# A row of 1,024 gains through DRAM: one write and one broadcast read in place of eight transposes in a hybrid block

## The chip, the cores and the metric

The kernel runs on one core of one Trainium2 chip. The metric is the device time of one execution in microseconds (us). Before the change it is 730.49 us, the median of three runs (730.33 to 730.49).

## The reference, cut to what matters

One backbone layer over 512 latent tokens of width 1,024, with 256 context tokens. A modulation vector gives shift, scale and gate; the normed input goes through one wide projection; a gated convolution and a neighbourhood attention of 16 heads are projected, merged through two gates, projected once more, normed and added to the input:

```
sh, sc, gt = _modulation(c, w_mod[i], b_mod[i])
h = _rmsnorm(x, pre_g[i]) * (1.0 + sc[:, None, :]) + sh[:, None, :]
parts = _split_in(h @ w_in[i])
...
merged = sigmoid(g_a) * y_a + sigmoid(g_b) * y_b
y = merged @ w_o
x = x + gt[:, None, :] * _rmsnorm(y, post_g[i])
```

The last line is what the change touches: each of the 1,024 output columns is multiplied by `gt * post_g` of that column. Both are vectors over columns, the same for every token.

## The kernel before, in words

All matmuls are on TensorE (PE) in fp32r, with operands split into a high part (a ScalarE cast, L70) and a low part (a VectorE subtraction, L71); a projection of one unit is three matmuls (L115, L116, L117) for each of eight slices of the contraction. Weights come in chunks of two DMAs of 512 KB each (`Chunk`, L84, tile `raw`, two buffers), issued by SyncE (SP) one chunk ahead of their use.

The work has these stages:

- **Start and context.** Modulation columns, norm, the first projection with its weights, then context keys and convolutions 0 to 3. `gain(k)` (L447 to L455) computes eight columns of the gate as a [128, 8] tile, `gains`: column 128k + p of the model lies in partition p, place k. L466 multiplies them with the post norm weight.
- **Eight pairs of heads** (the loop at L664). `blocks` holds for each pair two heads with four blocks of 128 queries; eight slots a pair. Each slot takes pieces of the projections listed in `plan` (keys and queries, values, convolutions, gates), then scores, softmax, transposes and the product with the values. The bias tile `bt` is loaded for each half pair (L543).
- **Merge** (the loop at L710). For j = 0 to 7 the two branch projections of unit j are multiplied with their gates and added; merge gates of unit j + 2 follow (L719). At j = 5 the products of gate and post norm weight are brought from [128, 8] columns to a tile that every partition holds in full, `gpost` [128, 1024]: eight copies on VectorE spread a column over 128 places (L730, tile `ta`), eight transposes on PE against the identity turn each so that every partition has the row (L731), and two ScalarE copies empty the two PSUM banks (L732). At j = 6 the output projection's first half of weights is loaded and split (`load_wo`, L705, tile `wo`).
- **Output projection** (L745 on). PE multiplies (L754); ScalarE sums the squares (L759), VectorE multiplies with `gpost` (L760); after the norm's root VectorE scales and adds `x` (L791), and the result is stored (L794).

Outside a part of the start that is written as a manual schedule, the framework orders each engine's instructions: an instruction is placed when its inputs and its buffers are ready, with the order of the program as priority. So one can run far ahead of its place in the text. Each engine and each DMA queue then works in that order. PSUM banks of the merge come in turn from eight (`pj`); tiles of the merge's pool `bp`, `gpost` among them, take the memory that the attention's pool `aw` gives back.

Of the kernel before, what the change touches and what calls it, by code (L numbers as in the profile page):

```python
# [9 lines left out]
F32 = mybir.dt.float32  # L10
# [5 lines left out]
P = 128  # L16
D = 1024
KT = 8
S = 512
# [8 lines left out]
def layer(ctx: ExitStack, tc, xp, ctxt, ctxT, cc, wmod, small, wfirst, win, wout, wo, rel, tab, out):  # L28
    nc = tc.nc
# [3 lines left out]
    wp = ctx.enter_context(tc.tile_pool(name="wp", bufs=2))  # L33
    cv = ctx.enter_context(tc.tile_pool(name="cv", bufs=2))
    pp = ctx.enter_context(tc.tile_pool(name="pp", bufs=1, space=bass.MemoryType.PSUM))

    class Banks:

# [9 lines left out]
    ident = const.tile([P, P], F32, name="ident")  # L48
# [4 lines left out]
    gains = const.tile([P, KT], F32, name="gains")  # L53
# [13 lines left out]
    def split(H, L, src, scale=None):  # L67

        if scale is None:
            nc.scalar.copy(H, src)  # L70
            nc.vector.tensor_sub(L, src, H.bitcast(F32))  # L71
        else:
            nc.scalar.mul(H, src, scale)
            nc.vector.scalar_tensor_tensor(
                out=L, in0=src, scalar=scale, in1=H.bitcast(F32), op0=ALU.mult, op1=ALU.subtract
            )
# [150 lines left out]
    pj = Banks(0, 1, 2, 3, 4, 5)  # L227

    def unit(w, i, m=hx):
        ps = pj()  # L230
        proj_T(ps, w, i, m)
        return ps
# [346 lines left out]
    def turn2(pts, b, TH, TL):  # L579
        tps = [psT().rearrange("p (c q) -> p c q", c=4) for _ in pts]  # L580
        for tp, pt in zip(tps, pts):
            for c in range(4):
                nc.tensor.transpose(tp[:, c], pt[:, c * P:(c + 1) * P], ident)  # L583
        for n, tp in enumerate(tps):
            split(TH[:, b + n], TL[:, b + n], tp)

    def gather(p, h, TH, TL):
        r, q = (lo, hi)[h], (hi, lo)[h]
        o = psO()
        o3 = o.rearrange("p (b q) -> p b q", b=4)  # L590

        work = [(4, slice(0, 4), lambda t: t[:, :, 2]), (5, slice(0, 4), lambda t: t[:, :, 3])]
        work.append((0, slice(0, 4, 3), lambda t: t[:, 0:4:3, 0]))
        for k in range(1, 3):
            work.append((k, slice(k - 1, k + 1), lambda t, k=k: t.rearrange("p b c q -> p (b c) q")[:, 4 * k - 3:4 * k + 1:3]))
        work.append((3, slice(2, 4), lambda t: t[:, 2:4, 1]))
        for n, (kt, dst, src) in enumerate(work):
            for t in (TH, TL):
                nc.tensor.matmul(  # L599
                    o3[:, dst], lhsT=V[p][:, kt, h], rhs=src(t),  # L600
                    start=n == 0 and t is TH, stop=n == len(work) - 1 and t is TL,
                )
        tmp = aw.tile([P, S], F32, name="tmp", bufs=1)
        nc.scalar.copy(tmp[r], o[q])
        nc.vector.tensor_add(attn[p][r, 64:512], o[r, :448], tmp[r, :448])
        nc.vector.tensor_add(attn[p][r, 0:64], o[r, 448:], tmp[r, 448:])
# [19 lines left out]
    def merge_gates(j):  # L626
        w = chunk()
        G[j] = []
        for i in range(2):
            n = 2 * j + i  # L630
            g = hp.tile([P, S], F32, name=f"g{n}", tag=f"hc{n % 8}")
            nc.scalar.activation(g, unit(w, i), AF.Tanh, scale=0.5)  # L632
            G[j].append(g)
            yield

    def chain(*gs):
        for g in gs:
            yield from g
# [24 lines left out]
    done = 0  # L663
    for i, (p, h, b) in enumerate(blocks):  # L664
        slot = i % 8
        if slot == 0:
            items = chain(*(g for g, _ in fill[p]))
            total, done = sum(n for _, n in fill[p]), 0
        upto = -(-total * (slot + 1) // 8)
        while done < upto:  # L670
            next(items)
            done += 1
        if T is not None and b == 0:
            gather(*T)
        if i + 2 < len(blocks):
            pts[i + 2] = scores(*blocks[i + 2])
        if b == 0:
            TH = aw.tile([P, 4, 4, P], F32R, name="TH", bufs=1)
            TL = aw.tile([P, 4, 4, P], F32R, name="TL", bufs=1)
            T = p, h, TH, TL  # L680

        if b % 2:
            turn2([pts.pop(i - 1), pts.pop(i)], b - 1, TH, TL)
# [7 lines left out]
    pj = Banks(*range(8))  # L691
# [9 lines left out]
    def load_wo(c, H, L):  # L701

        for i in range(4):
            raw = wp.tile([P, 2, S], F32, name="raw", bufs=2)
            nc.sync.dma_start(raw, wo[c, :, 2 * i:2 * i + 2])  # L705
            for k in range(2):
                split(H[2 * i + k], L[2 * i + k], raw[:, k])
        return H, L

    for j in range(KT):  # L710
        w = chunk()
        g = G[j]
        for i in range(2):
            nc.vector.scalar_tensor_tensor(  # L714
                out=g[i], in0=g[i], scalar=1.0, in1=unit(w, i, ua[i]), op0=ALU.add, op1=ALU.mult
            )
        nc.vector.tensor_add(g[0], g[0], g[1])
        split(mm[0][j], mm[1][j], g[0], 0.5)
        if j < 6:  # L719
            for _ in merge_gates(j + 2):  # L720
                pass
        if j == 5:

            gpost = bp.tile([P, D], F32, name="gpost")
            for i in range(2):
                gb = cv.tile([P, S], F32, name="ta")
                ps = pj()
                for k in range(4):
                    n = 4 * i + k
                    nc.vector.tensor_copy(gb[:, k * P:(k + 1) * P], gains[:, n:n + 1].broadcast_to([P, P]))  # L730
                    nc.tensor.transpose(ps[:, k * P:(k + 1) * P], gb[:, k * P:(k + 1) * P], ident)  # L731
                nc.scalar.copy(gpost[:, i * S:(i + 1) * S], ps)  # L732
        if j == 6:

            t = [hp.tile([P, 2, S], F32R, name=f"wo{i}", tag=f"h{i}") for i in range(8)]
            wos = [load_wo(0, [x[:, i] for x in t[:4] for i in range(2)], [x[:, i] for x in t[4:] for i in range(2)])]
# [8 lines left out]
    for c in range(2):  # L745
        H, L = wos[c]
        cs = slice(c * S, (c + 1) * S)
        ps = [pj() for t in range(4)]
# [129 lines left out]
```

## Time and profile before

| | |
|---|---|
| median of three runs | 730.49 us |
| profiled execution | 730.42 us |
| its span, first to last instruction | 728.6 us |
| granted TensorE clock, mean | 0.999 |
| PE busy | 716.9 us |
| VectorE (DVE) busy | 515.2 us |
| ScalarE (ACT) busy | 331.9 us |
| HBM read and written | 83.93 MB and 2.10 MB |

The profile is of one execution; 1.8 us lie outside its span. Rows of instructions name line, engine, operation, output and inputs; a row of the DMA queue of SyncE is named SPq. In the chain that ended last, each piece starts when what it waited for was done, so its starts give the pace of the engine, while busy times of matmuls overlap one another.

### The profile page before, as it was taken

What the parts mean: (1) busy time and instruction counts of PE and PEld (TensorE: products, weight loads), DVE (VectorE), ACT (ScalarE), POOL (GpSimd) and SP (SyncE); (2) the same over time, 40 slices, a digit from 0 to 9 for tenths busy, and PEclk for the clock granted to TensorE, in tenths of its full rate; (3) what the DMA queues carried; (4) which work ended last, traced back from release to release, by engine and by line L of the source; (5) the groups of instructions that cost most, each with busy time, mean ns of one, the idle gap of its engine ahead of it and who ended that gap; (6) DMA issues with size and microseconds to landing.
All of it is one profiled execution on the core that took longest, in us unless ns stands there. A gap on an engine that the chain in (4) does not pass through costs nothing.

```text
span 728.6 us, 9358 instructions
## 1 busy us (share of the span) xinstructions
PE 716.9 (98%) x3512; PEld 601.9 (83%) x3512; DVE 515.2 (71%) x1060; ACT 331.9 (46%) x619; POOL 0.7 (0%) x6
## 2 busy tenths in 40 slices
PE   7999999999999999999999999999999999999996
PEld 4888888888888888888888888888888888888885
DVE  6979999996998968879879779675844324335323
ACT  6564533563464654555536446434823213314221
POOL 0000000000000000000000000000000000000000
PEclk9999999999999999999999999999999999999999
DMA  8984973223212222121322212322133133235402
GB/s 343 406 305 175 317 269 121 96 67 99 72 60 73 72 74 73 58 88 57 116 73 73 73 58 73 98 77 73 58 115 109 65 116 103 71 116 181 165 10 107
DMA packets 25967, 86.63 MB, mean 119 GB/s; under 512 B 3009, under 2 KB 3393, under 8 KB 25922
## 3 DMA queue, kind: packets, MB, share of 16 engines
q1 hardware_dynamic: 25778, 85.84, 34.0%
q8 instruction: 27, 0.44, 0.2%
q10 hardware_dynamic: 144, 0.20, 0.1%
q14 instruction: 18, 0.15, 0.1%
HBM read 83.93 MB, written 2.10 MB: 118 GB/s over the span
## 4 chain that ended last, share of the span: by engine, by line
PE 96%; DVE 1%; DMA 1%; ACT 1%; SPq 0%; issue 0%; DVEq 0%; ACTq 0%
PE ps L115 20%; PE ps L117 20%; PE ps L116 20%; PE ps L128 6%; PE ps L754 6%; PE ps L599 4%; PE ps L583 4%; PE ps L133 3%; PE ps L551 3%; PE ps L141 2%; PE ps L307 2%; PE ps L311 2%; PE ps L308 2%; DMA wm<-in_wmod 1%; PE ps L560 1%; PE ps L146 1%
## 5 line engine op out<-in xcount | busy, mean ns | idle before, releaser
L115 PE MATMUL ps<-h,w 128*128 128x512 f32 x528 | 207.5, 393 | 0.0
L117 PE MATMUL ps<-h,w 128*128 128x512 f32 x528 | 206.0, 390 | 0.0
L116 PE MATMUL ps<-h,w 128*128 128x512 f32 x528 | 205.7, 390 | 0.0
L71 DVE TENSOR_TENSOR w<-raw,w 128x1024 fp32r<-128x1024 f32 (+1 forms) x98 | 113.1, 1173 | 58.9 <-ACT w L70 58.7
L70 ACT CAST w<-raw 128x1024 fp32r<-128x1024 f32 (+1 forms) x98 | 96.9, 1016 | 93.4 <-PE ps L117 64.6
L117 PEld LDWEIGHTS ps<-h,w 128*128 128x128 f32 x528 | 99.1, 188 | 20.9
L116 PEld LDWEIGHTS ps<-h,w 128*128 128x128 f32 x528 | 99.2, 188 | 20.2
L115 PEld LDWEIGHTS ps<-h,w 128*128 128x128 f32 x528 | 99.2, 188 | 20.1
L574 ACT ACTIVATE pt<-ps,m 128x512 f32<-128x512 f32 x64 | 44.3, 694 | 59.0 <-DVE m L571 59.0
L567 DVE CUSTOM_DVE_ANT_1 ps<-ps,bt 128x512 f32<-128x512 f32 x56 | 38.6, 700 | 15.1 <-PE ps L551 12.0
L71 DVE TENSOR_TENSOR TL<-ps,TH 128x512 fp32r<-128x512 f32 x64 | 42.7, 680 | 5.2 <-ACT TH L70 5.2
L714 DVE SCALAR_TENSOR_TENSOR g<-g,ps 128x512 f32<-128x512 f32 x16 | 11.0, 687 | 42.3 <-PE ps L117 42.3
L70 ACT CAST TH<-ps 128x512 fp32r<-128x512 f32 x64 | 35.1, 588 | 6.6 <-PE ps L583 6.4
L632 ACT ACTIVATE g<-ps 128x512 f32<-128x512 f32 x16 | 9.6, 598 | 59.6 <-PE ps L117 59.6
L583 PE MATMUL ps<-ident,pt 128*128 128x128 f32 x256 | 33.3, 272 | 0.0
L128 PE MATMUL ps<-w,h 128*128 128x512 f32 x128 | 32.7, 395 | 0.0
L576 DVE TENSOR_SCALAR pt<-pt,z 128x512 f32<-128x512 f32 x64 | 30.8, 482 | 1.0
L583 PEld LDWEIGHTS ps<-ident,pt 128*128 128x128 f32 x256 | 29.4, 140 | 2.3
L599 PE MATMUL ps<-TH,V 128*128 128x256 f32 (+1 forms) x96 | 28.5, 319 | 0.0
L599 PE MATMUL ps<-TL,V 128*128 128x256 f32 (+1 forms) x96 | 27.7, 318 | 0.0
L516 ACT ACTIVATE qd<-ta 64x512 fp32r<-64x512 f32 x32 | 20.2, 631 | 14.3 <-PE ps L560 7.6
L128 PEld LDWEIGHTS ps<-w,h 128*128 128x128 f32 x128 | 23.1, 189 | 4.3
(158 smaller groups left out, 1133.1 us busy)
## 6 DMA issues: line engine op xcount, KB each, us to landing
raw<-in_win SPq DMA_DIRECT2D x74, 512.0 KB, 4.2
wm<-in_wmod SPq DMA_DIRECT2D x34, 512.0 KB, 6.8
raw<-in_wout SPq DMA_DIRECT2D x16, 512.0 KB, 4.0
bt<-in_rel SPq DMA_DIRECT2D x16, 256.0 KB, 2.6
raw<-in_wo SPq DMA_DIRECT2D x8, 512.0 KB, 3.7
fraw<-in_wfirst SPq DMA_DIRECT2D x8, 384.0 KB, 8.1
x<-in_xp SPq DMA_DIRECT2D x4, 512.0 KB, 5.3
xr<-in_xp SPq DMA_DIRECT2D x4, 512.0 KB, 5.9
```

The costliest lines, as they stand in the source:

```text
L70: nc.scalar.copy(H, src)
L71: nc.vector.tensor_sub(L, src, H.bitcast(F32))
L115: nc.tensor.matmul(ps, lhsT=H[:, k, cs], rhs=mH[k], start=k == 0, stop=False)
L116: nc.tensor.matmul(ps, lhsT=H[:, k, cs], rhs=mL[k], start=False, stop=False)
L117: nc.tensor.matmul(ps, lhsT=L[:, k, cs], rhs=mH[k], start=False, stop=k == KT - 1)
L128: nc.tensor.matmul(ps, lhsT=mH[k][:, ts], rhs=both[:, k].rearrange("p a c -> p (a c)"), start=k == 0, stop=False, skip_group_check=True,)
L567: nc.vector.tensor_tensor_reduce(out=s3, in0=s3, in1=bt[:, e::4 - e][:, 0:2], scale=1.0, scalar=-3.0e38, op0=ALU.add, op1=ALU.max, accum_o ...
L574: nc.scalar.activation(pt, s, AF.Exp, bias=m, scale=1.0, accum_out=z)
L576: nc.vector.tensor_scalar(out=pt, in0=pt, scalar1=z, scalar2=None, op0=ALU.mult)
L583: nc.tensor.transpose(tp[:, c], pt[:, c * P:(c + 1) * P], ident)
L599: nc.tensor.matmul(o3[:, dst], lhsT=V[p][:, kt, h], rhs=src(t), start=n == 0 and t is TH, stop=n == len(work) - 1 and t is TL,)
L754: nc.tensor.matmul(ps, lhsT=mm[m][k][:, ts], rhs=w[k][:, cols], start=k + o == 0, stop=k == KT - 1 and o == 2)
```

## The change

The columns `gains` are written once to a DRAM tile of one row, `grow`, in an order that makes column 128k + p of the row from partition p, place k. The write stands in the loop over blocks at pair 4 (the fifth), slot 1. At j = 5 of the merge `gpost` is read from that row into all 128 partitions by one DMA. The eight copies, the eight transposes, the two PSUM banks and the two ScalarE copies are gone. Both DMAs are on SyncE's queue.

```diff
+    dr = ctx.enter_context(tc.tile_pool(name="dr", bufs=1, space=bass.MemoryType.DRAM))
...
     for i, (p, h, b) in enumerate(blocks):
         slot = i % 8
+        if (p, slot) == (4, 1):
+
+            grow = dr.tile([1, D], F32, name="grow")
+            nc.sync.dma_start(grow.rearrange("o (k p) -> p (o k)", p=P), gains)
         if slot == 0:
...
         if j == 5:
 
             gpost = bp.tile([P, D], F32, name="gpost")
-            for i in range(2):
-                gb = cv.tile([P, S], F32, name="ta")
-                ps = pj()
-                for k in range(4):
-                    n = 4 * i + k
-                    nc.vector.tensor_copy(gb[:, k * P:(k + 1) * P], gains[:, n:n + 1].broadcast_to([P, P]))
-                    nc.tensor.transpose(ps[:, k * P:(k + 1) * P], gb[:, k * P:(k + 1) * P], ident)
-                nc.scalar.copy(gpost[:, i * S:(i + 1) * S], ps)
+            nc.sync.dma_start(gpost, grow.broadcast_to([P, D]))
```

## The prediction

> **What bounds the kernel now.** I read the page first: its busy times, its DMA queues, its chain. Then the stages (the table of windows), the chain between 655 and 657 us, and the rows of the lines that the change removes.
>
> ```profile
> span 728.6 us, 9358 instructions
> PE 716.9 (98%) x3512; PEld 601.9 (83%) x3512; DVE 515.2 (71%) x1060; ACT 331.9 (46%) x619; POOL 0.7 (0%) x6
> ...
> q1 hardware_dynamic: 25778, 85.84, 34.0%
> q10 hardware_dynamic: 144, 0.20, 0.1%
> ```
>
> ```profile
> 118.00:190.00 72.00, 72.00 (x375) 61.59 (x374) 62.46 (x140) 37.39 (x77) 0.00 (x0) 1.00 0.27 89
> 190.00:202.00 12.00, 11.59 (x62) 9.68 (x62) 11.39 (x28) 6.26 (x13) 0.00 (x0) 1.00 0.32 103
> 202.00:320.00 118.00, 118.00 (x642) 101.80 (x641) 98.67 (x242) 64.72 (x142) 0.00 (x0) 1.00 0.23 74
> ...
> 470.00:515.00 45.00, 45.00 (x227) 37.86 (x226) 29.32 (x72) 20.25 (x39) 0.00 (x0) 1.00 0.21 71
> 515.00:640.00 125.00, 125.00 (x557) 103.69 (x556) 53.58 (x67) 40.19 (x57) 0.00 (x0) 1.00 0.29 97
> ...
> 656.00:678.50 22.50, 22.50 (x105) 18.75 (x104) 10.80 (x15) 10.43 (x18) 0.00 (x0) 1.00 0.64 224
> ```
>
> The columns of the second fence are the stretch, its length, and the busy time (with instructions) of PE, PE's weight loads, DVE, ACT and POOL, then clock, DMA share and GB/s. PE fills every one of these stretches but 190 to 202 us, where 0.41 us are idle. So TensorE is the bound: what leaves PE shortens the kernel, what leaves DVE or ACT does not, and a DMA costs only where PE in the end waits for what it holds up.
>
> **What the change removes.**
>
> ```profile
> 655.69 0.23 PE ps L117
> 655.92 0.87 PE ps L731 x8
> 656.79 0.23 PE ps L115
> ```
>
> ```profile
> L730 DVE COPY ta<-gains x8: 209/217/219, 474.8 to 492.9; 128x128 f32<-128x128 f32 x8
> ...
> L732 ACT COPY gpost<-ps 128x512 f32<-128x512 f32 x2 | 1.1, 594 | 0.0
> ```
>
> The first fence is the chain that ended last (start, length, what). The eight transposes stand in it with 0.87 us, between the last matmul of one projection and the first of the next, 0.23 us each. Without them L115 starts at 655.92 instead of 656.79: **0.87 us off the path**. I do not use the 272 ns that one transpose is busy; eight of those overlap. The eight copies, 8 x 0.217 = 1.74 us of DVE, ran at 475 to 493 us, where DVE is idle for 45 - 29.32 = 15.7 us and PE is full: nothing. The two ACT copies, 2 x 0.594 = 1.19 us, ran from 656.4 us, beside PE, with ACT idle for half of that stretch: nothing. The two PSUM banks come from eight taken in turn, and no wait of PE stands in the merge: nothing.
>
> Is the 0.87 us kept to the end? The next things that could be late are the weights of the output projection.
>
> ```profile
> 678.57 43.84 PE ps L754 x216
> ...
> 671.70 0.69 DVE L71 TENSOR_TENSOR wo<-raw,wo 128x512 fp32r<-128x512 f32 x1
> ...
> 687.38 1.29 DVE L71 TENSOR_TENSOR w<-raw,w 128x512 fp32r<-128x512 f32 x2 [1.21 <-ACT w L70]
> 699.04 0.69 DVE L760 TENSOR_TENSOR ys<-ps,gpost 128x512 f32<-128x512 f32 x1 [10.37 <-ACT sq L759]
> ```
>
> The first half's weights are split by 671.70 + 0.69 = 672.39, and PE begins with them at 678.57: 6.2 us to spare. The second half's are done at 688.7 and begin after 96 of the 216 matmuls, at about 678.57 + 43.84 x 96 / 216 = 698.1 (an estimate by share; the last 48 are of half width, so it comes somewhat later): over 9 us to spare. Against 0.87 us both hold.
>
> **What it adds: the read.** One DMA of 512 KB, in 128 rows of 4 KB, the shape of a weight load.
>
> ```profile
> raw<-in_win SPq DMA_DIRECT2D x74, 512.0 KB, 4.2
> ...
> bt<-in_rel SPq DMA_DIRECT2D x16, 256.0 KB, 2.6
> ...
> xr<-in_xp SPq DMA_DIRECT2D x4, 512.0 KB, 5.9
> ```
>
> ```profile
> 515.37 1.47 SPq L84 DMA_DIRECT2D raw<-in_win  x2
> 531.16 1.46 SPq L84 DMA_DIRECT2D raw<-in_wout  x2
> ...
> 647.65 1.46 SPq L84 DMA_DIRECT2D raw<-in_wout  x2
> 659.75 7.81 SPq L705 DMA_DIRECT2D raw<-in_wo  x4
> ```
>
> It takes 4.2 to 5.9 us by these rows (all 128 rows come from one place in DRAM, which no row here prices; I keep 5.9 as the upper end). Its first reader is L760 at 699.04. It may be issued as early as the attention's memory is free, shortly after 515 us, or as late as its place in the text, about 655 us. In the queue there are gaps of 14 us and 11 us at those places. At the worst it is put among the L705 loads, ahead of the first; these and the splits behind them (on ACT the cast waits, on DVE what follows it) come up to 5.9 us later, and 672.39 + 5.9 = 678.3 is still ahead of 678.57. With PE 0.87 us earlier the two would just cross for the last split, which belongs to a later slice of the contraction than the first matmuls need. Price: nothing, and at most some tenths of a microsecond in the worst place.
>
> **What it adds: the write.** 128 partitions with eight values each, and neighbours of one partition lie 512 bytes apart in the row. So the 4 KB go out as 1,024 pieces of 4 bytes, 64 for each of 16 engines. No DMA of the trace has such pieces. By q1's row a packet takes on average 0.340 x 16 x 728.6 / 25778 = 0.154 us at 3.3 KB; by q10's row (0.1%, so 0.05 to 0.15) 0.001 x 16 x 728.6 / 144 = 0.081 us at 1.4 KB. 64 pieces come to 9.9 us by the one and 5.2 us by the other. As the lower end I take the bias load, 2.6 us in all. I take 5.2 us, by the row with the smaller packets. The Trainium skill, "DMA: Bandwidth & Descriptors", section "Rules for kernel authors", speaks against this form: a DMA whose last dimension is strided becomes one descriptor for each element, and it says to make that dimension contiguous. No run here shows it yet; if it holds, the write is 1,024 descriptors instead of the 128 of a contiguous form, and the queue behind it is what can be late.
>
> When the write goes out is not fixed by the text. The copies of L730 stand in the text beside the transposes, and ran 655.92 - 492.9 = 163 us and more before them, as soon as their buffers were free. The write needs only `gains`, ready after L466:
>
> ```profile
> 116.71 0.80 SPq L543 DMA_DIRECT2D bt<-in_rel  x2
> 118.74 15.64 SPq L84 DMA_DIRECT2D raw<-in_win  x4
> ...
> 117.20 0.16 DVE L466 TENSOR_TENSOR gains<-gains,sp 128x8 f32<-128x8 f32 x1
> ...
> 123.05 1.05 ACT L70 CAST w<-raw 128x1024 fp32r<-128x1024 f32 x1 [10.13 <-DMA raw<-in_win]
> ...
> 129.17 1.22 DVE L71 TENSOR_TENSOR w<-raw,w 128x1024 fp32r<-128x1024 f32 x1
> ...
> 132.76 1.22 DVE L71 TENSOR_TENSOR w<-raw,w 128x1024 fp32r<-128x1024 f32 x1
> ...
> 138.23 0.39 PE L115 MATMUL ps<-h,w 128*128 128x512 f32 x1
> ```
>
> ```profile
> 329.79 0.33 SPq L84 DMA_DIRECT2D raw<-in_win  x1
> 339.44 0.33 SPq L543 DMA_DIRECT2D bt<-in_rel  x1
> 348.47 11.83 SPq L84 DMA_DIRECT2D raw<-in_win  x4
> ```
>
> If it stays near its place, pair 4 begins about 330 us: SP issues nothing for 9.3 us there and one bias load in 18 us, so even 9.9 us hide. If it is moved to the front, it goes out at about 117.5 us, ahead of the weight loads from 118.74 on. Behind it on SP wait those loads; on ACT, in order, the cast at 123.05 and the query casts after it; on DVE the two splits. The splits are done at 130.39 and 133.98; PE takes the first half from 138.23 and the second, 12 matmuls of 0.23 us later, from 141.0. So 7.8 and 7.0 us of delay are free, and 5.2 us cost nothing there. Price: nothing in either place at 5.2 us; 9.9 - 7.0 = 2.9 us at the upper end in the early place.
>
> **The sum.** 730.42 - 0.87 = 729.55 for the profiled execution; the median lies 0.07 us above that execution, so **729.6 us** for the median, 0.12% less. A measurement of this kernel can tell about 0.2%, 1.46 us, from no change, so the forecast is "within".
>
> **The rivals.**
>
> *The write goes out early and holds up the weights (slower).* Its place is SP's queue at 117.5 us, its price is what the 64 pieces take beyond 7.0 us, and it decides from 109 ns a piece on. At 154 ns it is 730.49 + 2.9 - 0.87 = 732.5 us. For it: the copies ran far ahead of their place, and DVE and ACT take everything behind the late cast in order. Against it: 109 ns is above q10's row, and in the late place it costs nothing. 14 in 100. The page's rule, read as a warning of slow writes, points to this case.
>
> *The order elsewhere shifts and PE's one wait of the middle goes away (faster).*
>
> ```profile
> PEld ps L551 <- ACT pt L574: 0.8, 1, 0.8
> PE ps L551 <- ACT pt L574: 0.4, 1, 0.4
> ```
>
> This wait is at 201 us, where DVE is busy 11.39 of 12 us. A write among the loads, or 18 instructions fewer, can change the order that the framework makes for the engines. At most these 0.8 us come on top: 730.49 - 0.87 - 0.8 = 728.8 us. Against it: the removed instructions lie 270 us later, so only the early write reaches it. 10 in 100.
>
> *The gain is given back (no change).* An early or a late DMA eats a part of the 0.87 us, or the read collides with the output weights: 730.0 to 730.5 us. For it: DMA share 0.64 in the stretch from 656 us. Against it: over 6 us to spare. 10 in 100. That the transposes would remain in the program is excluded by the diff.
>
> **How the numbers follow.** The forecast has 66 in 100, with a range of its own from 729.3 to 729.9. The range reaches from the faster case's 728.8 to the slower case's 732.5. Within 0.2% (729.0 to 732.0) lie the forecast, the given-back gain and no part of the others: 0.76 less a little, since the order can change by more than I priced: 0.74. Faster has 0.12, slower 0.14.
>
> **What would show it.** Right: no L731, PE's busy time less by about 0.9 us, the chain with L117 and L115 0.23 us apart where the transposes stood, and L760 released by L759 as before. In the queue one DMA into `grow` with 1,024 packets and one of 512 KB into `gpost`. Wrong: a wait of PE between 138 and 205 us put down to weights, casts or banks; a DMA into `grow` that lands later than 10 us after its issue; a cast of L705's weights after 678 us.

## The result, and the profile after

The changed kernel takes 739.31 us (median of four runs, 737.36 to 739.79) against 730.46 us for the kernel before: a ratio of 1.0117, 95% interval 1.0105 to 1.0130. It is 8.85 us slower. The profiled execution took 739.41 us with a span of 737.6 us, 9.0 us longer than before.

The page of the changed kernel. Line numbers differ a little from those before: the projections are L116 to L118 instead of L115 to L117, the output projection is L752 instead of L754.

```profile
span 737.6 us, 9333 instructions
PE 721.0 (98%) x3504; PEld 604.8 (82%) x3504; DVE 514.4 (70%) x1052; ACT 331.0 (45%) x617; POOL 0.7 (0%) x6
...
PEclk9999999899999999999999999999999999999998
```

The eight transposes are gone (3,504 matmuls instead of 3,512), and the write shows in the DMA packets under 512 bytes: 4,065 instead of 3,009, and the 1,024 pieces of 4 bytes are among the 1,056 new ones. But PE is busy 4.1 us longer, and its clock has a dip in the eighth slice of 18 us, which it had not before. The stages and a finer cut of the place of the dip, from the table of windows (PE, its weight loads, DVE, ACT, POOL, clock, DMA share, GB/s):

```profile
118.00:190.00 72.00, 65.39 (x322) 55.40 (x322) 54.16 (x122) 32.54 (x68) 0.00 (x0) 0.95 0.34 88
...
134.00:139.00 5.00, 0.61 (x6) 0.41 (x5) 4.65 (x8) 3.98 (x7) 0.00 (x0) 1.00 0.00 0
139.00:144.00 5.00, 4.47 (x16) 3.67 (x16) 4.84 (x8) 2.40 (x7) 0.00 (x0) 0.66 0.31 107
...
146.00:150.00 4.00, 4.00 (x12) 3.10 (x11) 3.54 (x14) 3.50 (x11) 0.00 (x0) 0.57 0.10 37
```

Between 118 and 190 us PE has lost 6.6 us; before it was full there. It is nearly idle from 134 to 139 us and again from 144 to 146, and in the windows behind these two stops its mean clock is 0.66 and 0.57. The timelines of SyncE's queue, ScalarE, VectorE and PE show why (start, length, what, and in brackets the wait before it):

```profile
117.33 0.43 SPq L670 DMA_DIRECT2D grow<-gains  x1
118.51 34.68 SPq L85 DMA_DIRECT2D raw<-in_win  x6
...
132.62 1.05 ACT L71 CAST w<-raw 128x1024 fp32r<-128x1024 f32 x1 [19.60 <-DMA raw<-in_win]
137.85 0.37 ACT L153 COPY ta<-ps 128x256 f32<-128x256 f32 x1 [0.65 <-DVE qe L519]
...
138.40 0.41 DVE L154 TENSOR_TENSOR ta<-ta,ps 128x256 f32<-128x256 f32 x1
...
145.22 0.82 DVE L154 TENSOR_TENSOR ta<-ta,ps 128x256 f32<-128x256 f32 x2
...
117.59 1.98 PE L142 MATMUL ps<-hc,w 128*128 128x512 f32 x8
138.87 3.06 PE L129 MATMUL ps<-w,hc 128*128 128x512 f32 x8 [4.38 <-DVE ta L154]
145.70 0.50 PE L552 MATMUL ps<-ks,qd 128*128 128x512 f32 x1 [2.23 <-DVE ta L154]
159.69 0.40 PE L561 MATMUL ps<-ks,qd 128*128 128x256 f32 x2
```

In the chain that ended last, the output projection stands at

```profile
687.79 43.84 PE ps L752 x216
```

The write went out at 117.33 us, right after the gains were computed, not at the fifth pair. The weight load behind it took 14.0 us to land, against 4.2 to 5.0 us before. The cast that waits for it began at 132.62 instead of 123.05 us. Behind that cast in ScalarE's order stand the query casts and then L153, which together with L154 on VectorE empties the PSUM banks of the values' projection. PE wanted such a bank twice, for the last context unit (L129) and for the first scores (L552), and waited 4.38 and 2.23 us.

With the start of L142 (L141 before) as zero, the same points of the kernel before, from PE's timeline, are these; its output projection begins at 678.57:

```profile
117.78 1.52 PE L141 MATMUL ps<-hc,w 128*128 128x512 f32 x6
...
134.51 2.00 PE L128 MATMUL ps<-w,hc 128*128 128x512 f32 x8
...
137.30 0.40 PE L551 MATMUL ps<-ks,qd 128*128 128x512 f32 x1
149.57 0.40 PE L560 MATMUL ps<-ks,qd 128*128 128x256 f32 x2
```

The first scores come 19.52 us after zero before and 28.11 after: 8.59 us lost. The point at L560 comes at 31.79 and 42.10: 10.31 us lost. The output projection begins at 560.79 and 570.20: 9.41 us lost, so 0.90 us were won back on the way there, and the transposes stood on that way.

The 8.59 us are set by the bank of the first scores. L154, which empties it, starts 145.22 - 117.59 = 27.63 us after zero; before, it was 135.67 - 117.78 = 17.89 (L153, a row shown further down). That is 9.74 us later, and about 1.2 us of it were slack. The rows of ScalarE and VectorE from the cast to this L154 all stand 9.55 to 9.57 us later than before, so PE's pace did not set them. On PE the 8.59 us are its two waits, 6.61 us, and slower matmuls between them; a faster clock there would only have made the second wait longer (an inference). Behind the first scores another 10.31 - 8.59 = 1.72 us are lost at the lower clock: from 146 to 150 us PE is busy throughout at 0.57, which is 4.00 x 0.43 = 1.72 us.

The Trainium skill, "TensorE: Matmul & The Clock Gate", Part 1, says that the array falls to half its clock after about 3.4 us of idleness and returns after about as long a time of work. This trace agrees behind the first wait: after 4.38 us of waiting the next 5 us have a mean clock of 0.66. It does not agree behind the second: there 2.23 us of waiting were followed by 0.57 over 4 us. In finer windows the clock is near 0.50 from 139.7 to 143.2 us and from 146.6 to 150.0, about 3.4 us each time. The length of the wait alone does not decide in these runs: after a wait of 2.9 us in the run of one column below, and after one of 1.86 us in the run with the row turned first, the clock stayed at 1.00.

### The profile page after: what moved, and what is told of

It is laid out like the page before. It is cut to its first block, busy times and chain, and to the rows that moved or that the text cites. A ratio compares the mean times of both kernels' runs of the same rounds, so it can differ in the third digit from the quotient of the medians.

```text
span 737.6 us, 9333 instructions
## 1 busy us (share of the span) xinstructions
PE 721.0 (98%) x3504; PEld 604.8 (82%) x3504; DVE 514.4 (70%) x1052; ACT 331.0 (45%) x617; POOL 0.7 (0%) x6
## 2 busy tenths in 40 slices
DMA packets 27151, 87.15 MB, mean 118 GB/s; under 512 B 4065, under 2 KB 4449, under 8 KB 27106
## 4 chain that ended last, share of the span: by engine, by line
PE 87%; DVE 5%; DMA 4%; issue 2%; ACT 1%; SPq 0%; DVEq 0%; ACTq 0%
PE ps L118 18%; PE ps L116 18%; PE ps L117 18%; PE ps L752 6%; PE ps L129 4%; PE ps L600 4%; PE ps L584 4%; DMA raw<-in_win 4%; PE ps L552 3%; PE ps L134 2%; PE ps L308 2%; PE ps L312 2%; PE ps L142 2%; PE ps L309 2%; DVE w L72 1%
## 5 line engine op out<-in xcount | busy, mean ns | idle before, releaser
L116 PE MATMUL ps<-h,w 128*128 128x512 f32 x528 | 208.2, 394 | 0.0
L118 PE MATMUL ps<-h,w 128*128 128x512 f32 x528 | 206.5, 391 | 0.0
L117 PE MATMUL ps<-h,w 128*128 128x512 f32 x528 | 206.3, 391 | 0.0
L118 PEld LDWEIGHTS ps<-h,w 128*128 128x128 f32 x528 | 99.5, 188 | 21.1
L117 PEld LDWEIGHTS ps<-h,w 128*128 128x128 f32 x528 | 99.6, 189 | 20.4
L116 PEld LDWEIGHTS ps<-h,w 128*128 128x128 f32 x528 | 99.5, 189 | 20.2
L129 PE MATMUL ps<-w,h 128*128 128x512 f32 x128 | 32.7, 394 | 0.0
L519 DVE SCALAR_TENSOR_TENSOR qe<-ta,qd 64x512 fp32r<-64x512 f32 x32 | 21.9, 685 | 11.2 <-ACT qd L517 10.7
```

Source lines behind the costliest of these rows:

```text
L116: nc.tensor.matmul(ps, lhsT=H[:, k, cs], rhs=mH[k], start=k == 0, stop=False)
L117: nc.tensor.matmul(ps, lhsT=H[:, k, cs], rhs=mL[k], start=False, stop=False)
L118: nc.tensor.matmul(ps, lhsT=L[:, k, cs], rhs=mH[k], start=False, stop=k == KT - 1)
L129: nc.tensor.matmul(ps, lhsT=mH[k][:, ts], rhs=both[:, k].rearrange("p a c -> p (a c)"), start=k == 0, stop=False, skip_group_check=True,)
```

## The experiments

Theory 1, from the trace above: the 64 pieces of 4 bytes an engine, some 150 ns each, stand ahead of the weight loads of 118.5 us. Rivals: the write is dear wherever it stands; the read or the missing instructions with their new order are at fault.

**The write at its place.** The changed kernel keeps the last bias load's instruction, and the write is queued behind it:

```diff
-            nc.sync.dma_start(grow.rearrange("o (k p) -> p (o k)", p=P), gains)
+            with tc.issue_after(bias[-1]):
+                nc.sync.dma_start(grow.rearrange("o (k p) -> p (o k)", p=P), gains)
```

> The write is tied behind the bias load of its own pair, so that it goes out at about 330 us instead of 117 us; all else as in the changed kernel. Theory 1 (64 pieces an engine of about 150 ns stand ahead of the weight loads of 118.5 us in the queue): the write still takes about 10 us to land, but SP issues nothing large for 9 us or more behind it, PE has no wait at 134 to 146 us, and only the removed 0.87 us remain: 729.6 us (729.2 to 730.0). Theory 2 (the write costs wherever it stands, since weights are always in flight): a wait of PE of about 6 us near 340 us, 735 us or more. Theory 3 (not the write but the new order of the other instructions): 739 us again.

Measured: 728.56 us against 730.40; ratio 0.9978 (0.9969 to 0.9987). PE has no wait at 134 to 146 us. The queue:

```profile
287.34 0.43 SPq L672 DMA_DIRECT2D grow<-gains  x1
295.99 1.49 SPq L85 DMA_DIRECT2D raw<-in_win  x2
...
310.29 1.05 ACT L71 CAST w<-raw 128x1024 fp32r<-128x1024 f32 x1
```

The bias load of pair 4 is itself issued one pair early, so the write stands at 287 us, not 330. It still took 13.2 us to land, and the weight loads 8.65 us behind it took 8.0 us instead of the 4.0 to 4.9 of the same loads before. But ScalarE takes them up only at 310.29 us, so nobody felt it. The place decides, and the new order without the early write costs nothing: the second and third theories fall. The gain is larger than theory 1 gave (729.2 to 730.0 us): 0.87 us would be a ratio of 0.9988, just above the interval. The profile has 609.74 us from L142 to the end against 610.82, a gain of 1.08 us. The profiled execution, at 729.19 us, was the slowest of the eleven of this kernel, 0.63 us above their median, which accounts for most of the rest of the 1.84 us between the medians; what makes its executions differ is open.

**No write at all.** The read takes another row:

```diff
-            nc.sync.dma_start(gpost, grow.broadcast_to([P, D]))
+            nc.sync.dma_start(gpost, cc[0:1].broadcast_to([P, D]))
```

(and the write is taken out).

> The changed kernel with no write at all; the read takes the conditioning vector's row in place of the gains, so the output is not the reference's. It shows the removed transposes and the read alone: 729.6 us by the prediction's sum; if it equals the kernel with the late write, the late write costs nothing. Theory that the read or the missing instructions cost: 737 us or more.

Measured: 728.94 us against 730.05; ratio 0.9987 (0.9978 to 0.9996). By the profile 609.96 us from L142 to the end, 0.86 us less than before. The removed transposes are worth what the prediction said, the read is free, and the late write costs nothing that can be seen beside this run.

**The early write alone.** The kernel before, with the write added at the same place in the text and nothing reading the row.

```diff
+        if (p, slot) == (4, 1):
+            grow = dr.tile([1, D], F32, name="grow")
+            nc.sync.dma_start(grow.rearrange("o (k p) -> p (o k)", p=P), gains)
```

> The kernel before with the early write of 1,024 pieces added, and nothing that reads the row; copies and transposes stay. Theory 1: the whole loss of the changed kernel and 0.87 us more, 740.2 us (739.2 to 741). Theory that the read or the missing instructions are at fault: 730.5 us.

Measured: 742.11 us, ratio 1.0161 (1.0145 to 1.0176). The write carries the whole loss, and somewhat more than I expected: here it landed after 12.4 us instead of 10.5, the load behind it after 15.7, and PE waited 5.8 and 1.9 us.

**128 pieces of 32 bytes.** Early, with the row laid out partition by partition:

```diff
-grow.rearrange("o (k p) -> p (o k)", p=P)
+grow.rearrange("o (p k) -> p (o k)", p=P)
```

> The write stays early, at 117 us, but its row is laid out so that each partition writes its eight values side by side: 128 pieces of 32 bytes instead of 1,024 of 4. The columns of the row are then in another order, so the gains do not meet their columns and the output is not the reference's. Theory 1 by number of pieces: 8 an engine, about 1.2 us, less than any slack, so 729.6 us. Theory 2, it is the write to DRAM in the queue as such, or its completion, that holds up the loads behind it: 739 us. Theory 3 (order): 739 us, as the order is that of the changed kernel.

Measured: 728.97 us against 730.40, ratio 0.9984 (0.9975 to 0.9993). The write landed in 2.6 us and the load behind it in 4.2. So an early write to DRAM is no harm as such.

**Half of the write early.** Two writes, columns 0 to 511 at once and the others behind the bias load:

```diff
+            halves_ = [(grow[:, i * S:(i + 1) * S].rearrange("o (k p) -> p (o k)", p=P), gains[:, 4 * i:4 * i + 4]) for i in range(2)]
+            nc.sync.dma_start(*halves_[0])
+            with tc.issue_after(bias[-1]):
+                nc.sync.dma_start(*halves_[1])
```

> The write in two: columns 0 to 511 early (32 pieces an engine), columns 512 to 1,023 late, behind the bias load of pair 4. Theory 1 with 150 ns a piece: the cast at 123 us comes 4.8 us late. In the kernel before, the bank for the last context unit is free 5.2 us before PE wants it, so the first wait (4.4 us in the changed kernel) is gone; but the bank for the first scores is free only about 1.2 us before, so PE waits about 3.6 us there and then runs some microseconds at a lower granted clock: 733 to 735 us. If the loss were in proportion to the pieces: 730.46 - 0.87 + 9.7 / 2 = 734.4 us. If it had a threshold at 7.0 us of delay, as the prediction had it: 729.6 us.

Measured: 739.78 us, ratio 1.0138 (1.0122 to 1.0153). All three expectations fail, theory 1's price of a piece among them. With half the pieces, the first write landed after 11.3 us and the load behind it after 15.0, and PE waited 5.1 and 1.3 us. The late half, also 512 pieces, landed after 9.3 us. So the delay does not go by the number of pieces. What stayed the same is that 128 partitions write side by side into each row of 512 bytes.

The next runs add an early write that nothing reads to the kernel before, as in the write alone, and change only its shape: how many pieces, and how near they lie.

**1,024 pieces, each 512 bytes from the next.**

```diff
+            grow = dr.tile([P, KT, P], F32, name="grow")
+            nc.sync.dma_start(grow[:, :, 0], gains)
```

> The kernel before with an early write of 1,024 pieces of 4 bytes that nothing reads, as in the kernel with the write alone, but each piece goes to a block of 512 bytes of its own. After the half write, 64 pieces of 150 ns each no longer explains the delay. Theory by number of pieces or by their form: as with the write alone, 741 to 742 us. Theory of shared blocks (pieces that many engines write into the same few bytes of a row wait for one another): the loads behind it are not late, 730.4 us.

Measured: 731.58 us against 730.31, ratio 1.0015 (1.0006 to 1.0024). The same number of 4-byte pieces now landed in 3.9 us, and the load in 5.8. Number and form are not the price; how near the pieces lie is, or how small the area is that they fill (512 KB here, 4 KB in the change). A small loss is left, since the load still comes later than 4.2 us: PE waited 0.9 us for the bank of the first scores.

**One column, 128 pieces.**

```diff
+            grow = dr.tile([1, P], F32, name="grow")
+            nc.sync.dma_start(grow.rearrange("o p -> p o"), gains[:, 0:1])
```

> The kernel before with an early write of one column that nothing reads: 128 pieces of 4 bytes, one from each partition, into one row of 512 bytes. Theory by number of pieces: 8 an engine, 1.2 us, hidden, 730.4 us. Theory of a fixed price of 4-byte pieces, and theory of shared blocks with the rows at work side by side (128 pieces in a row, whether there are eight rows or one): about 10 us of delay, 740 to 742 us.

Measured: 738.04 us, ratio 1.0097 (1.0081 to 1.0114). An eighth of the pieces, packed side by side: 8.8 us to land, 11.6 for the load. Packed pieces are dear whatever their number, though a little less so than the 740 to 742 us expected.

**64 partitions, eight columns.**

```diff
+            grow = dr.tile([1, D], F32, name="grow")
+            nc.sync.dma_start(grow.rearrange("o (k p) -> p (o k)", p=P)[:64], gains[:64])
```

> The kernel before with an early write, unread, from partitions 0 to 63 with all eight columns: 512 pieces of 4 bytes, 32 an engine, as many as in the first half of the divided write, but 64 to a row of 512 bytes instead of 128. Fixed price: 741 us. Shared blocks, price by pieces in a row: about half the delay, 733 to 736 us. By number of pieces as the divided write showed it (512 pieces nearly as dear as 1,024): 739 to 741 us.

Measured: 738.65 us, ratio 1.0111 (1.0095 to 1.0126); 10.4 us to land. Half the pieces in a row of 512 bytes are not half as dear, so it is not the number in 512 bytes that counts. Side by side, 16 pieces fill 64 bytes in this run as in the one before.

**Pieces 64 bytes apart.**

```diff
+            grow = dr.tile([KT, P, 16], F32, name="grow")
+            nc.sync.dma_start(grow[:, :, 0].rearrange("k p -> p k"), gains)
```

> The kernel before with an early, unread write of 1,024 pieces of 4 bytes; the pieces of one column lie 64 bytes apart, so a block of 64 bytes holds one piece, and a block of 512 bytes holds eight, from eight neighbouring partitions. If what the pieces share and wait for is a block of 64 bytes or less: the weight load lands within about 6 us, as with pieces 512 bytes apart, 730.4 to 731.6 us. If it is a block of 512 bytes: 12 us or more to land, 736 to 742 us.

Measured: 731.73 us against 730.05, ratio 1.0026 (1.0015 to 1.0038); 4.7 us to land, 6.3 for the load, and PE waited 1.2 us. With one piece to 64 bytes the price is gone but for what is left with 512 bytes too. The Trainium skill, "DMA: Bandwidth & Descriptors", section "Specifications", gives 512 bytes as the least transfer for full rate, with a read and rewrite below it. That is a rule for the size of a transfer, and it does not explain these runs: all the shapes of 4-byte pieces are equally far below it and landed in 3.9 to 13.9 us. Nor is a distance of 512 bytes the border of this price: 64 bytes apart landed in 4.7 us and 512 bytes apart in 3.9.

**Eight pieces of one partition in 64 bytes.**

```diff
+            grow = dr.tile([P, 32], F32, name="grow")
+            nc.sync.dma_start(grow[:, 0:16:2], gains)
```

> The kernel before with an early, unread write of 1,024 pieces of 4 bytes; the eight pieces of one partition lie 8 bytes apart in 64 bytes of their own, and the next partition's 128 bytes further. So pieces share a block of 64 bytes only with pieces of the same partition. If pieces of one block wait for one another whoever writes them: about as dear as the changed kernel, 738 to 742 us. If only pieces of different partitions (different engines) do: 730.4 to 731.6 us.

Measured: 735.92 us, ratio 1.0082 (1.0068 to 1.0096); 6.8 us to land, 8.8 for the load. It lies between the two expectations. So packing costs also where the pieces that lie together all come from one partition, though less than with 16 pieces in 64 bytes from 16 partitions.

**The early write from ScalarE's queue.**

```diff
-            nc.sync.dma_start(grow.rearrange("o (k p) -> p (o k)", p=P), gains)
+            nc.scalar.dma_start(grow.rearrange("o (k p) -> p (o k)", p=P), gains)
```

> The changed kernel with the early write issued from ScalarE instead of SyncE, so that it is in another queue of the same 16 engines. If the weight loads are late because they stand behind the write in one queue, they are now served in between: 729 to 731 us. If the write blocks the engines themselves, whatever the queue: 737 us or more.

Measured: 739.38 us, ratio 1.0126 (1.0111 to 1.0141). From the timelines of ScalarE and SyncE:

```profile
117.52 0.40 ACTq L670 DMA_DIRECT2D grow<-gains  x1
132.37 1.05 ACT L71 CAST w<-raw 128x1024 fp32r<-128x1024 f32 x1 [18.97 <-DMA raw<-in_win]
...
118.87 21.23 SPq L85 DMA_DIRECT2D raw<-in_win  x3
```

The write and the loads are in two queues; the write landed after 13.9 us, and the load still took 13.4. So it is not its place in a queue that delays the load; something that the two queues share is held, the DMA engines or the memory. In the changed kernel the DMA engines' busy share is 0.52 from 125 to 130 us, while they move only 20 GB/s; before, a share of 0.60 from 120 to 125 us went with 201 GB/s.

**The row turned first.** Early, but as 8 pieces of 512 bytes, after one transpose. These lines stand right behind the computation of the gains, and the write in the loop is gone:

```diff
+        grow = dr.tile([1, D], F32, name="grow")
+        turned = pj()
+        nc.tensor.transpose(turned[:KT, :P], gains, ident)
+        grows = const.tile([KT, P], F32, name="grows")
+        nc.scalar.copy(grows, turned[:KT, :P])
+        nc.sync.dma_start(grow.rearrange("o (k p) -> (o k) p", p=P), grows)
```

> The changed kernel with another form of the same write, as early as before: one transpose on PE turns the gains to 8 partitions by 128, ScalarE empties the bank, and the write has 8 pieces of 512 bytes that share no block. The output is the reference's. Theory of shared blocks: no late load, and the gain of the late write less one transpose of 0.1 us: 728.7 to 729.8 us. If any early write is at fault: 737 us or more. A wait of SP for the transpose could cost up to 1 us.

Measured: 731.15 us against 730.05, ratio 1.0017 (1.0008 to 1.0026).

```profile
117.94 0.27 PE L470 MATMUL ps<-ident,gains 128*8 128x128 f32 x1 [1.86 <-DVE gains L467]
...
118.00:123.00 5.00, 5.00 (x27) 4.31 (x28) 4.93 (x9) 0.26 (x1) 0.00 (x0) 1.00 0.83 240
```

The load behind the write lands in 4.3 us, so this form of the write is harmless. But PE takes its instructions in order, and the transpose waited 1.86 us for the gains: more than the 0.87 us that the change wins. I had left that wait of PE out.

What the shapes show together, with the time to land of the write and of the weight load issued behind it, and PE's two waits for banks together (each row from one profiled execution; the change's own write took 10.5 to 13.9 us in four kernels, so small differences between rows say little):

| early write | pieces | in 64 bytes | write lands, us | load lands, us | PE waits, us |
|---|---|---|---|---|---|
| none (before) | | | | 4.2 to 5.0 | 0 |
| 32-byte pieces | 128 | 2 | 2.6 | 4.2 | 0 |
| 512 bytes apart | 1,024 | 1 | 3.9 | 5.8 | 0.9 |
| 64 bytes apart | 1,024 | 1 | 4.7 | 6.3 | 1.2 |
| own partition | 1,024 | 8 | 6.8 | 8.8 | 3.8 |
| one column | 128 | 16 | 8.8 | 11.6 | 6.7 |
| 64 partitions | 512 | 16 | 10.4 | 13.4 | 5.8 |
| the change | 1,024 | 16 | 10.5 | 14.0 | 6.6 |
| first half | 512 | 16 | 11.3 | 15.0 | 6.4 |
| the change's write alone | 1,024 | 16 | 12.4 | 15.7 | 7.7 |

Down the table it is the third column, not the second, that goes with the fourth. But 64 bytes is only one way to count nearness, and another was not separated from it: the runs of 1,024 pieces that are further apart also fill a larger area, 16 KB (own partition), 64 KB and 512 KB instead of 4 KB. No run spreads groups of pieces that share 64 bytes over a large area. So it is shown that packed 4-byte pieces are slow and pieces 64 bytes apart are not; whether blocks of 64 bytes, blocks of another size or the area decide, and what happens inside the engines or the memory, stays open.

## Why the prediction was wrong

- **The gain: right.** 0.87 us for the transposes; 0.90 us in the trace, 0.86 us in the run without a write. The read is free, as said; it was issued at 527 us, in the gap that the prediction named. It took 7.2 us to land, more than the 4.2 to 5.9 us of the prediction, but its first reader starts only at 708 us (L758).
- **That the write may run ahead of its place: right, and weighed too low.** The prediction gave the exact place, 117.5 us ahead of the loads of 118.74, and a rival of 14 in 100. The copies that ran 163 us ahead of their text were evidence enough to expect it, since the gains have no buffer to wait for.
- **The duration of the write: the first step that failed.** I took 5.2 us from q10's row, with 9.9 us as the upper end. It lands in 10.5 us, and the load behind it lets the cast start 9.57 us late. The upper end met the size, but by chance: 64 pieces times the mean packet time is not the mechanism, and the means mix sizes: 3,009 of the 25,967 packets before are under 512 bytes. 1,024 pieces take 3.9 us when they lie apart, and 128 take 8.8 us when they lie together.
- **The slack: the step that failed most, and the one that alone would have put the time outside the range.** "So 7.8 and 7.0 us of delay are free" looked only at the two weight splits. I named the cast that everything on ScalarE waits behind, and did not follow what that everything is. L152 and L153 before the change empty the banks. The bank of the last context unit was free at 128.84 + 0.41 = 129.25 us, 5.3 us before PE wanted it at 134.51 (L128), and the bank of the first scores only about 1.2 us before:

```profile
128.84 0.41 DVE L153 TENSOR_TENSOR ta<-ta,ps 128x256 f32<-128x256 f32 x1
...
135.67 0.82 DVE L153 TENSOR_TENSOR ta<-ta,ps 128x256 f32<-128x256 f32 x2
```

  The first of the two at 135.67 ends near 136.1 us (an estimate, half of the pair), and L551 starts at 137.30. In the table PE already waits 0.9 us where the load lands in 5.8 us instead of 4.2 to 5.0. My own upper end of 9.9 us with this slack would have given 9.9 - 1.2 = 8.7 us of loss instead of 2.9; the trace has 8.59 us at that point. The measured delay of 9.74 us with the slack of 7.0 us would have lost only 2.7 us, inside the range; the predicted 5.2 us with the slack of 1.2 us would already have lost 4.0.
- **The clock: not priced at all.** Behind the first scores it costs 1.72 us on top of the 8.59 us of the late bank. With the 0.90 us won back, that makes the 9.41 us at the output projection.
- **The rival "order shifts, PE's wait of the middle goes away"** did not come: the wait of 0.4 us for the exponentials (L551 before, L552 in the changed kernel) is in every profile.

The version to keep is the one with the write at its place: 0.9978 (0.9969 to 0.9987) of the kernel before, and some 10.8 us less than the change as it stood (728.56 and 739.31 us, from two comparisons).

## What to carry to other kernels

Where a framework orders the instructions, a DMA without a buffer to wait for goes out as soon as its data are there; look for what stands behind it at that moment, and tie it down if that is dear. When a load may come late, follow the waiting engine's order to its end: here not the weights but the emptying of PSUM banks had the least slack, 1.2 us. Before counting the pieces of a small write to DRAM, lay them apart (64 bytes apart was enough here) or make them longer (32 bytes was enough for 128 pieces).

## What the runs showed that I had not expected

4-byte pieces that lie side by side in DRAM take about 9 to 14 us to land whether there are 1,024, 512 or 128 of them (10.5 to 13.9, 9.3 to 11.3 and 8.8 us), while 1,024 pieces 64 bytes apart land in 4.7 us and 128 pieces of 32 bytes in 2.6. Another queue does not help: the load behind still took 13.4 us.
